# One decoder block in fp32: convolution taps loaded in rows of 512 bytes, latent columns split 352 and 352, last sums first on VectorE

## The chip, the cores and the metric

The kernel runs on one core of one Trainium2 chip. The metric is the device time of one execution in microseconds, the median over the runs. On the core, TensorE (PE) multiplies, VectorE (DVE), ScalarE (ACT) and GpSimd (POOL) do elementwise work, and SyncE (SP) issues the DMAs that bring data from HBM.

## The reference

One decoder layer on 512 tokens of width 1024, all in float32. An adaptive norm makes `h` from `x`; one input projection of `h` yields the columns of the GLU (2 x 1024), the latents of attention (384 for q, 256 for k and v, 64 for the rotary key, together 704) and the gates of the two branches (2 x 1024). Branch A is GLU, causal depthwise convolution with 31 taps, layer norm, swish and a projection; branch B is latent attention with eight heads. Both are gated, added and projected by `w_out`. Then comes an MLP of width 4096.

```
mod = silu(c) @ W_ada + b_ada                    # shift, scale, gate, twice
h = rms_norm(x, g_pre_mix) * (1 + scale1) + shift1
z = h @ w_in
u_glu, q_lat, kv_lat, k_r, gate_logits = split(z)
u = ua * sigmoid(ub)
u = causal_depthwise_conv(u, conv_w, conv_b)     # conv_w: 31 x 1024
y_a = silu(layer_norm(u)) @ w_conv_out
q = rms_norm(q_lat) @ w_uq ; kv = rms_norm(kv_lat) @ w_ukv
y_b = attention(q, kv, rope(k_r)) @ w_attn_out
y = (sigmoid(g_A) * y_a + sigmoid(g_B) * y_b) @ w_out
x = x + gate1 * rms_norm(y, g_post_mix)
h = rms_norm(x, g_pre_mlp) * (1 + scale2) + shift2
x = x + gate2 * rms_norm(square(relu(h @ w_mlp_in)) @ w_mlp_out, g_post_mlp)
```

## The kernel before

Each fp32 product is made of three matmuls in a faster format (`mm3`): every operand is split into a high half (a cast, on ScalarE) and a low half (the difference, on VectorE), and TensorE adds high x high, high x low and low x high. High and low halves lie in one large SBUF tile, `r_arena`; raw fp32 data, weights just loaded among it, lie in another, `f_arena`. Places in both are taken and given back during the kernel, so a load can only be issued when the data that had its place before has been used. The results of TensorE go through eight PSUM banks.

No instruction is issued where it is written. A planner records all of them, computes their dependences and orders each engine's queue, and `issue` sends them out, so nearly all instructions have line L388 in the profile. TensorE follows the program order. The other queues, SP's DMAs included, go by due time: an instruction's due time comes from the matmuls that depend on it, less costs on the way, and `plan.hurry` pulls those recorded under it forward (`HG` is 3e3, in ns). The key is

```
return (o.rank, o.i) if o.eng == "pe" else (o.dead - o.hurry, o.i)
```

Buffer places are chosen over eight passes from the times of the last plan. Any change of a cost or a size can so move rows in other places. DMAs share a ring of eight semaphores: the ninth waits for the landing of the first.

The stages in order: the adaLN vectors and the first projection, group by group over the input rows (`first_products`, groups k=0 to 7); eight transposes of the taps `cwr` into `cw`, which has channels on partitions; the latents (`lat_gemm`); the GLU tiles; attention over eight heads, with 240 tap multiply-adds of the convolution between its steps on VectorE (`pump`); the projection of attention; layer norm; the projections of both branches; the gates; `w_out`; the MLP in four chunks, each with a second gemm after Strassen, whose products the function `banked` adds into accumulators in `f_arena`; the last norm and the output. Late adaLN rows (`w_ada`) are accumulated on VectorE during layer norm and `w_out`.

In `lat_gemm` weights come in units (`wunit`: a DMA, a cast, a subtraction). The first 512 columns take four units of 2 x 512, in four open banks, one for each block of 128 tokens; the other 192 take two units of 4 x 192, one block after the other.

Of the kernel before, what the change touches and what calls it, by code (L numbers as in the profile page):

```python
# [15 lines left out]
ALU = mybir.AluOpType  # L16
# [376 lines left out]
def tile_hybrid_block(  # L393
# [48 lines left out]
    def emit(past, replay):  # L442
# [122 lines left out]
        pos4 = tile_of([NT, P], I32, "pos4")  # L565
        pos4f = tile_of([NT, P], F32, "pos4f")
        sp.dma_start(out=pos4, in_=positions[0].rearrange("(a p) -> a p", p=P))
        cwr = fa.alloc(D)
        sp.dma_start(out=fa.v(cwr)[:TAPS, :], in_=conv_w)
        plan.hurry = 0.0  # L570

        bc = pb.alloc()
# [53 lines left out]
        def hs(k, a=0, n=T):  # L626
            return ra.v(hT[k][0])[:, a:a + n], ra.v(hT[k][1])[:, a:a + n]
# [96 lines left out]


        cw = tile_of([P, KD, TAPS], F32, "cw")
        for ct in range(KD):
            pe.transpose(pb.v(bc)[:, 128 + ct * 32:128 + ct * 32 + TAPS], fa.v(cwr)[:TAPS, ct * P:(ct + 1) * P],
                         ident[:TAPS, :TAPS])
        dve.tensor_scalar(cw, pb.v(bc)[:, 128:384].rearrange("p (a b) -> p a b", b=32)[:, :, :TAPS], 0.5, None, ALU.mult)  # L730
        fa.free(cwr)
        pb.free(bc)

# [84 lines left out]
        kraw = fa.alloc(NT * DR)  # L818

        def lat_gemm():  # L820
            lb = [pb.alloc() for _ in range(NT)]
            for k0 in range(0, KD, 2):
                w = wunit(w_in, k0, C_QL, 2, 512)
                for k in range(2):
                    for t in range(NT):
                        mm3(pb.v(lb[t]), hs(k0 + k, t * P, P), w(k, 0, 512), k0 + k == 0, k0 + k == KD - 1)
                w.free()
                pump(PUMPS[0])
            for t in range(NT):
                b = fa.alloc(640)  # L830
                act.copy(fa.v(b)[:, 0:512], pb.v(lb[t]))
                latF.append(b)
            pb.free(*lb)
            ws = [wunit(w_in, kh, C_R2, 4, 192) for kh in (0, 4)]
            for t in range(NT):
                b = pb.alloc()
                for k in range(KD):
                    mm3(pb.v(b, 192), hs(k, t * P, P), ws[k // 4](k % 4, 0, 192), k == 0, k == KD - 1)
                act.copy(fa.v(latF[t])[:, 512:640], pb.v(b, 128))
                act.copy(fa.v(kraw)[:, t * DR:(t + 1) * DR], pb.v(b, 192)[:, 128:192])  # L840
                pb.free(b)
            for w in ws:
                w.free()
            pump(PUMPS[0])
# [678 lines left out]
        for ch in range(NCH):  # L1523
            hid = fa.alloc(HPC * T)
            hv = fa.v(hid, "p (k t) -> p k t", k=HPC)
            GRP = 4 if ch == 0 else 2
            for n0 in range(0, HPC, GRP):
                bs = [pb.alloc() for _ in range(GRP)]
                ws = ws0 if ch == 0 and n0 == 0 else hid_weights(ch * HPC + n0, GRP)
                step = 256 if ch == 0 and n0 == 0 else T  # L1530
                for t0 in range(0, T, step):
                    for i in range(GRP):
                        for k in range(KD):
                            mm3(pb.v(bs[i])[:, t0:t0 + step], ws[i - i % 2, k // 4](k % 4, (i % 2) * P, P), h2s(k, t0, step),
                                k == 0, k == KD - 1)
                for w in ws.values():
                    w.free()
                for i in range(GRP):
                    r = fa.alloc(T)
                    act.activation(fa.v(r), pb.v(bs[i]), AF.Relu)  # L1540
                    act.activation(hv[:, n0 + i], fa.v(r), AF.Square)
                    fa.free(r)
                    pb.free(bs[i])
                if ch >= NCH - 2:
                    take(late, ADAS[1])
            if ch == NCH - 1:
                for p_ in h2:
                    ra.free(*p_)
                take(late)
                G2 = gate_row(5, g_post_mlp, 1.0)  # L1550
                fin = [stat(4) for _ in range(NT)]
            if ch == 0:
                ysb = [fa.alloc(D) for _ in range(NT)]
            seen = {}

            def banked(mi, nh, bs):
                n = seen[mi, nh] = seen.get((mi, nh), 0) + 1
                done = n == (1 if (mi, nh) == (1, 0) else 2)
                sl = slice(nh * 512, (nh + 1) * 512)
                for tt in range(2):  # L1560
                    t = 2 * mi + tt
                    y = fa.v(ysb[t])[:, sl]
                    if ch == 0 and n == 1:
                        act.copy(y, pb.v(bs[tt]))
                    else:
                        dve.tensor_tensor(y, pb.v(bs[tt]), y, ALU.add)
                    if ch < NCH - 1 or not done:
                        continue
                    s = fin[t]
# [65 lines left out]
```

## Time and profile before

| | |
|---|---|
| median of 3 runs | 834.04 us (833.59 to 836.13) |
| profiled execution | 832.68 us |
| its span, first to last instruction | 830.9 us |
| granted TensorE clock, mean | 0.994 |
| TensorE busy | 805.1 us, 97% |
| VectorE busy | 686.6 us, 83% |
| ScalarE busy | 422.4 us, 51% |
| data moved by DMA | 117.28 MB, mean 141 GB/s |

Busy time is the time in which the engine executes; the rest of the span it waits. The profile names, for each wait, the instruction of another engine that ended last before it (the releaser). In the timeline a row is a start, a length, the engine, the operation and the count of equal ones, and in brackets the idle time before them. In the window view each engine has its busy time and count in the window; then come the granted clock, the mean busy share of the 16 DMA engines and the rate.

### The profile page before, as it was taken

Reading aid. Unit: us, or ns where it says so; the run is one execution under the profiler, and the core shown is the slowest. Engines: PE = TensorE matmul, PEld = TensorE weight load, DVE = VectorE, ACT = ScalarE, POOL = GpSimd, SP = SyncE. Lnnn points to the kernel's source line nnn. Section 1 sums busy time; section 2 is a strip of 40 time slices with the busy share of each in tenths; the row PEclk is TensorE's granted clock in tenths of the full one; section 3 lists DMA queues with packets and bytes.
Section 4 is the critical chain, followed back from the end, with each engine's and each line's share of the span. In section 5 each row is a group of like instructions: output and inputs, shape, how many; then the busy total and the mean of one; then the engine's idle time right before and its main releaser. Section 6 shows DMA issues by size and latency. Waiting matters only on the chain.

```text
span 830.9 us, 10647 instructions
## 1 busy us (share of the span) xinstructions
PE 805.1 (97%) x3940; PEld 672.5 (81%) x3940; DVE 686.6 (83%) x1012; ACT 422.4 (51%) x712; POOL 26.4 (3%) x84
## 2 busy tenths in 40 slices
PE   6989999999999999999999989999999999999995
PEld 3867888889987888888877879888888888888884
DVE  4979989999999999998999589298529993975696
ACT  5364273275884356218424387375346354554642
POOL 2001020000000000000000020000000000000001
PEclk9999999999999999999999999999999999999998
DMA  9998423201464140062799362065014831660302
GB/s 309 321 301 261 153 70 95 71 27 44 135 176 116 40 126 26 26 229 76 277 341 374 118 205 79 27 195 160 0 51 149 277 131 52 193 212 1 102 0 103
DMA packets 86824, 117.28 MB, mean 141 GB/s; under 512 B 7275, under 2 KB 60628, under 8 KB 86771
## 3 DMA queue, kind: packets, MB, share of 16 engines
q1 hardware_dynamic: 86770, 116.59, 43.6%
q8 instruction: 31, 0.51, 0.2%
q14 instruction: 23, 0.18, 0.1%
HBM read 108.18 MB, written 8.39 MB: 140 GB/s over the span
## 4 chain that ended last, share of the span: by engine, by line
PE 87%; DVE 6%; DMA 4%; ACT 2%; issue 1%; POOL 0%; POOLq 0%; DVEq 0%; ACTq 0%; SPq 0%
PE psum L388 87%; DVE f_arena L388 4%; DMA f_arena<-in_w_in_dram 2%; DVE r_arena L388 1%; ACT f_arena L388 1%; DMA f_arena<-in_w_out_dram 1%; ACT r_arena L388 1%; POOL stats L388 0%; DMA f_arena<-in_x_dram 0%; DMA f_arena<-in_w_ada_dram 0%; ACT stats L388 0%; POOLq L1630 0%; DVE mod L388 0%; DVEq L1630 0%; DVE cols L388 0%
## 5 line engine op out<-in xcount | busy, mean ns | idle before, releaser
L388 PE MATMUL psum<-r_arena 128*128 128x512 f32 (+3 forms) x3592 | 765.7, 373 | 8.5 <-ACT r_arena L388 3.6
L388 PEld LDWEIGHTS psum<-r_arena 128*128 128x128 f32 x3592 | 631.3, 189 | 126.8 <-ACT r_arena L388 4.9
L388 DVE TENSOR_TENSOR r_arena<-f_arena,r_arena 128x1024 fp32r<-128x1024 f32 (+4 forms) x232 | 248.1, 1093 | 97.2 <-PE psum L388 56.2
L388 ACT CAST r_arena<-f_arena 128x1024 fp32r<-128x1024 f32 (+4 forms) x222 | 209.3, 967 | 189.7 <-PE psum L388 123.5
L388 DVE SCALAR_TENSOR_TENSOR f_arena<-f_arena,cw 128x512 f32<-128x512 f32 x240 | 164.5, 748 | 0.0
L388 ACT ACTIVATE f_arena<-psum 128x512 f32<-128x512 f32 x64 | 38.1, 598 | 131.4 <-PE psum L388 124.6
L388 DVE TENSOR_TENSOR f_arena<-f_arena 128x1024 f32<-128x1024 f32 (+3 forms) x78 | 77.3, 1006 | 5.5 <-ACT f_arena L388 3.6
L388 ACT ACTIVATE f_arena<-f_arena 128x512 f32<-128x512 f32 (+3 forms) x100 | 58.5, 606 | 13.5 <-DVE f_arena L388 12.6
L388 DVE SCALAR_TENSOR_TENSOR f_arena<-f_arena,cT 128x256 f32<-128x256 f32 (+2 forms) x84 | 55.3, 705 | 0.2
L388 PE MATMUL psum<-ident,f_arena 128*128 128x128 f32 (+1 forms) x240 | 34.4, 283 | 7.5 <-DVE f_arena L388 7.5
L388 PEld LDWEIGHTS psum<-ident,f_arena 128*128 128x128 f32 (+1 forms) x240 | 28.9, 146 | 12.8 <-DVE f_arena L388 8.2
L388 DVE TENSOR_TENSOR f_arena<-psum,f_arena 128x512 f32<-128x512 f32 x52 | 35.4, 687 | 4.4 <-PE psum L388 4.3
L388 ACT CAST r_arena<-psum 128x512 fp32r<-128x512 f32 (+2 forms) x57 | 30.3, 567 | 16.6 <-PE psum L388 16.4
L388 DVE TENSOR_TENSOR r_arena<-psum,r_arena 128x512 fp32r<-128x512 f32 (+2 forms) x57 | 35.7, 658 | 2.5 <-ACT r_arena L388 1.9
L388 POOL TENSOR_TENSOR stats<-stats,nhalf 128x1 f32<-128x1 f32 x24 | 16.8, 708 | 485.4 <-ACT stats L388 485.4
L388 ACT COPY f_arena<-psum 128x512 f32<-128x512 f32 (+4 forms) x42 | 19.9, 501 | 22.1 <-PE psum L388 21.9
L388 ACT ACTIVATE r_arena<-f_arena 128x512 fp32r<-128x512 f32 (+3 forms) x20 | 13.0, 648 | 18.7 <-DVE f_arena L388 16.2
L388 DVE CUSTOM_DVE_ANT_0 f_arena<-psum,mask 128x128 f32<-128x128 f32 (+3 forms) x32 | 15.2, 487 | 2.6 <-PE psum L388 2.5
L388 DVE SCALAR_TENSOR_TENSOR f_arena<-f_arena 128x512 f32<-128x512 f32 (+1 forms) x18 | 13.4, 747 | 0.3
L388 DVE SCALAR_TENSOR_TENSOR f_arena<-f_arena,psum 128x512 f32<-128x512 f32 x16 | 11.0, 685 | 3.1 <-PE psum L388 2.6
L388 DVE TENSOR_SCALAR f_arena<-f_arena,stats 128x1024 f32<-128x1024 f32 x8 | 6.0, 752 | 8.4 <-POOL stats L388 8.4
L388 DVE SCALAR_TENSOR_TENSOR f_arena<-psum,stats,f_arena 128x512 f32<-128x512 f32 x8 | 5.6, 748 | 8.5 <-POOL stats L388 8.3
(94 smaller groups left out, 188.0 us busy)
## 6 DMA issues: line engine op xcount, KB each, us to landing
f_arena<-in_w_ada_dram SPq DMA_DIRECT2D x16, 1024.0 KB, 8.2
f_arena<-in_w_mlp_in_dram SPq DMA_DIRECT2D x32, 512.0 KB, 4.3
f_arena<-in_w_mlp_out_dram SPq DMA_DIRECT2D x32, 512.0 KB, 5.2
f_arena<-in_w_in_dram SPq DMA_DIRECT2D x28, 512.0 KB, 4.7
f_arena<-in_x_dram SPq DMA_DIRECT2D x8, 512.0 KB, 8.0
f_arena<-in_w_ada_dram SPq DMA_DIRECT2D x16, 256.0 KB, 5.7
f_arena<-in_w_ada_dram SPq DMA_DIRECT2D x8, 512.0 KB, 6.4
h_spill<-r_arena SPq DMA_DIRECT2D x16, 256.0 KB, 4.1
```

The source lines that it names most:

```text
L388: getattr(self.real[o.eng], o.fn)(*o.a, **o.k)
```

## The change

Three edits.

The taps, 31 rows of 1024 floats, are read as 248 rows of 128 floats (512 bytes) by three DMAs, of 112, 128 and 8 rows. The buffer has 256 words per partition and no longer 1024. Two transposes (128 x 128 and 128 x 120) take the place of eight (31 x 128), and the scaling into `cw` reads them in another stride.

The 704 latent columns are done as 352 and 352: four units of 2 x 352 for each half.

In the last chunk of the MLP, what `banked` records has `plan.hurry` at `HG`; the body moves to `add_block`, unchanged.

```
-        cwr = fa.alloc(D)
-        sp.dma_start(out=fa.v(cwr)[:TAPS, :], in_=conv_w)
+        cwr = fa.alloc(2 * P)
+        cw_rows = conv_w.rearrange("t (a p) -> (t a) p", p=P)
+        for r0, r1, at in ((0, P, 0), (P, P + 112, 0), (P + 112, TAPS * KD, 112)):
+            c0 = P if r0 else 0
+            sp.dma_start(out=fa.v(cwr)[at:at + r1 - r0, c0:c0 + P], in_=cw_rows[r0:r1])
...
-        for ct in range(KD):
-            pe.transpose(pb.v(bc)[:, 128 + ct * 32:128 + ct * 32 + TAPS], fa.v(cwr)[:TAPS, ct * P:(ct + 1) * P],
-                         ident[:TAPS, :TAPS])
-        dve.tensor_scalar(cw, pb.v(bc)[:, 128:384].rearrange("p (a b) -> p a b", b=32)[:, :, :TAPS], 0.5, None, ALU.mult)
+        for i, n in enumerate((P, TAPS * KD - P)):
+            pe.transpose(pb.v(bc)[:, (1 + i) * P:(1 + i) * P + n], fa.v(cwr)[:n, i * P:(i + 1) * P], ident[:n, :n])
+        dve.tensor_scalar(cw, pb.v(bc)[:, P:P + TAPS * KD].rearrange("p (b a) -> p a b", a=KD), 0.5, None, ALU.mult)
...
+            NL = (QL + KL + DR) // 2
...
-                w = wunit(w_in, k0, C_QL, 2, 512)
+                w = wunit(w_in, k0, C_QL, 2, NL)
...
-            ws = [wunit(w_in, kh, C_R2, 4, 192) for kh in (0, 4)]
+            ws = [wunit(w_in, kh, C_QL + NL, 2, NL) for kh in range(0, KD, 2)]
...
             def banked(mi, nh, bs):
+                plan.hurry = HG if ch == NCH - 1 else 0.0
+                add_block(mi, nh, bs)
+                plan.hurry = 0.0
```

The planner's order changes with it. Three places matter here.

First SP's queue at the first projection, where the taps are loaded. `in_conv_w_dram` are the taps; the loads of 128x4x128 are the weights of groups k=6 and k=7, those of 128x4x256 GLU weights, those of 128x2x512, 128x4x192 and 128x2x352 latent weights. Before:

```order
L388 DMA pos_96<-in_positions_dram 4x128
L388 DMA f_arena<-in_conv_w_dram 31x1024
L388 DMA f_arena<-in_w_in_dram 128x4x128 x2
L388 DMA f_arena<-in_w_in_dram 128x2x512 x3
L388 DMA f_arena<-in_w_in_dram 128x4x192
```

After, with the tap load of 112 rows standing some 25 rows further up:

```order
L388 DMA pos_96<-in_positions_dram 4x128
L388 DMA f_arena<-in_conv_w_dram 128x128
L388 DMA f_arena<-in_conv_w_dram 8x128
L388 DMA f_arena<-in_w_in_dram 128x4x256
L388 DMA f_arena<-in_w_in_dram 128x4x128 x2
L388 DMA f_arena<-in_w_in_dram 128x4x256
L388 DMA f_arena<-in_w_in_dram 128x2x352 x4
```

The one tap load became three, and a GLU load moved ahead of the weights of k=6 and k=7.

Second SP's queue ahead of the `w_out` gemm. `in_x_dram` is the residual, `in_w_ada_dram` a late adaLN load. Before:

```order
L388 DMA f_arena<-in_x_dram 128x1024
L388 DMA f_arena<-in_w_ada_dram 128x2x1024
L388 DMA f_arena<-in_x_dram 128x1024 x2
L388 DMA f_arena<-in_w_out_dram 128x2x512
L388 DMA f_arena<-in_w_ada_dram 128x2x1024
L388 DMA f_arena<-in_w_out_dram 128x2x512
```

After:

```order
L388 DMA f_arena<-in_x_dram 128x1024
L388 DMA f_arena<-in_w_out_dram 128x2x512
L388 DMA f_arena<-in_w_ada_dram 128x2x1024
L388 DMA f_arena<-in_x_dram 128x1024 x2
L388 DMA f_arena<-in_w_out_dram 128x2x512
L388 DMA f_arena<-in_w_ada_dram 128x2x1024
L388 DMA f_arena<-in_w_out_dram 128x2x512
```

The first `w_out` load moved ahead of one adaLN load and two residual loads, and the others follow earlier by about one place.

Third VectorE's queue at the end. A sum from `psum` into the accumulator is one of the gemm's last; a row with `stats` is a norm's last product. Before:

```order
L388 TENSOR_TENSOR f_arena<-psum,f_arena 128x512 x2
L388 TENSOR_TENSOR f_arena<-f_arena 128x512
L388 SCALAR_TENSOR_TENSOR f_arena<-f_arena,stats 128x512 x2
L388 TENSOR_TENSOR f_arena<-f_arena 128x512
L388 SCALAR_TENSOR_TENSOR f_arena<-f_arena,stats 128x512 x2
L388 TENSOR_TENSOR f_arena<-psum,f_arena 128x512
```

After:

```order
L388 TENSOR_TENSOR f_arena<-psum,f_arena 128x512
L388 SCALAR_TENSOR_TENSOR f_arena<-f_arena,stats 128x512 x2
L388 TENSOR_TENSOR f_arena<-f_arena 128x512
L388 SCALAR_TENSOR_TENSOR f_arena<-f_arena,stats 128x512 x2
L388 TENSOR_TENSOR f_arena<-psum,f_arena 128x512 x2
L388 TENSOR_TENSOR f_arena<-f_arena 128x512
```

The last sum from `psum` stood behind the norm of two other token blocks and now stands right behind the sum before it.

More of the change, by code (lines that the diff above doesn't have):

```diff
@@ L820, in lat_gemm @@
         def lat_gemm():
+            NL = (QL + KL + DR) // 2
             lb = [pb.alloc() for _ in range(NT)]
             for k0 in range(0, KD, 2):
-                w = wunit(w_in, k0, C_QL, 2, 512)
+                w = wunit(w_in, k0, C_QL, 2, NL)
                 for k in range(2):
                     for t in range(NT):
-                        mm3(pb.v(lb[t]), hs(k0 + k, t * P, P), w(k, 0, 512), k0 + k == 0, k0 + k == KD - 1)
+                        mm3(pb.v(lb[t], NL), hs(k0 + k, t * P, P), w(k, 0, NL), k0 + k == 0, k0 + k == KD - 1)
                 w.free()
@@ L829, in lat_gemm @@
             for t in range(NT):
-                b = fa.alloc(640)
-                act.copy(fa.v(b)[:, 0:512], pb.v(lb[t]))
+                b = fa.alloc(QL + KL)
+                act.copy(fa.v(b)[:, 0:NL], pb.v(lb[t], NL))
                 latF.append(b)
             pb.free(*lb)
-            ws = [wunit(w_in, kh, C_R2, 4, 192) for kh in (0, 4)]
+            ws = [wunit(w_in, kh, C_QL + NL, 2, NL) for kh in range(0, KD, 2)]
             for t in range(NT):
@@ L837, in lat_gemm @@
                 for k in range(KD):
-                    mm3(pb.v(b, 192), hs(k, t * P, P), ws[k // 4](k % 4, 0, 192), k == 0, k == KD - 1)
-                act.copy(fa.v(latF[t])[:, 512:640], pb.v(b, 128))
-                act.copy(fa.v(kraw)[:, t * DR:(t + 1) * DR], pb.v(b, 192)[:, 128:192])
+                    mm3(pb.v(b, NL), hs(k, t * P, P), ws[k // 2](k % 2, 0, NL), k == 0, k == KD - 1)
+                act.copy(fa.v(latF[t])[:, NL:QL + KL], pb.v(b, QL + KL - NL))
+                act.copy(fa.v(kraw)[:, t * DR:(t + 1) * DR], pb.v(b, NL)[:, QL + KL - NL:])
                 pb.free(b)
@@ L1556, in banked, with add_block @@
             def banked(mi, nh, bs):
+                plan.hurry = HG if ch == NCH - 1 else 0.0
+                add_block(mi, nh, bs)
+                plan.hurry = 0.0
+            def add_block(mi, nh, bs):
                 n = seen[mi, nh] = seen.get((mi, nh), 0) + 1
```

## The prediction

> **What bounds the kernel now.** I read the page's first and fourth part, then the waits of TensorE, then the timeline round each wait. Busy time and the chain of waits come first.
>
> ```profile
> PE 805.1 (97%) x3940; PEld 672.5 (81%) x3940; DVE 686.6 (83%) x1012; ACT 422.4 (51%) x712; POOL 26.4 (3%) x84
> ...
> PE 87%; DVE 6%; DMA 4%; ACT 2%; issue 1%; POOL 0%; POOLq 0%; DVEq 0%; ACTq 0%; SPq 0%
> ...
> PE psum L388 <- ACT r_arena L388: 3.6, 3, 2.4
> PE psum L388 <- DVE r_arena L388: 2.4, 4, 0.9
> ```
>
> TensorE carries 87% of the chain. So only three things shorten the kernel: fewer or shorter matmul slots, a wait of TensorE that goes, and the stretch after the last matmul. The two waits quoted are those the change can reach; the rest of this text finds where they stand. The profiled execution took 832.68 us, 1.36 below the median of the runs (834.04); the sum is made against 832.68 and 1.36 is added at the end.
>
> **Latent columns, 512 and 192 made into 352 and 352.** The rows give what one matmul costs back to back.
>
> ```profile
> L388 PE MATMUL psum<-r_arena 128*128 128x192 f32 x96 | 10.9, 274 | 0.0
> ...
> 492.24 7.68 PE L388 MATMUL psum<-r_arena 128*128 128x256 f32 x62
> ...
> 783.34 38.25 PE L388 MATMUL psum<-r_arena 128*128 128x512 f32 x168
> ```
>
> The first row is from the groups by shape, the others are of the timeline (start, length, count). 512 columns: 38.25/168 = 228 ns. 256: 7.68/62 = 124 ns. 192: 10.9/96 = 114 ns, hardly less than 256, so the narrow half pays for columns that it doesn't have. Before: 96 x 228 + 96 x 114 = 32.8 us. After: 192 matmuls of 352, a width that no row shows. Cheapest, in proportion to 512: 157 ns, 30.1 us (-2.7). Dearest, on the line from 192 to 512: 171 ns, 32.8 us (0). I take the line from 256 to 512, its nearest neighbours: 163 ns, 31.3 us, **-1.5 us**. All of it is on TensorE's path. The two extra weight units cost ScalarE and VectorE nothing new in bytes, only starts; VectorE's other work covers them, and if it didn't they would show as waits on r_arena in that gemm.
>
> **Tap transposes, eight made into two.**
>
> ```profile
> 70.80 0.67 PE L388 MATMUL psum<-ident,f_arena 31*128 31x31 f32 x8
> 71.40 1.89 PE L388 MATMUL psum<-r_arena 128*128 128x512 f32 x7
> ...
> 499.76 1.47 PE L388 MATMUL psum<-ident,f_arena 128*128 128x128 f32 x12
> ```
>
> The eight hold TensorE from 70.80 to 71.40, 0.60 us. Two full ones at 1.47/12 = 122 ns are 0.24: **-0.35 us** (bounds 0 and -0.4).
>
> **The tap load, one of 31 rows made into three of 112, 128 and 8.** The window view (busy times, then DMA share and GB/s last) and the timeline show the cost.
>
> ```profile
> 44.00:46.00 2.00, 1.94 (x8) 1.47 (x9) 2.00 (x8) 2.00 (x4) 0.00 (x0) 1.00 1.15 316
> 46.00:48.00 2.00, 2.00 (x12) 1.69 (x12) 2.00 (x6) 0.96 (x2) 0.00 (x0) 1.00 0.49 128
> 48.00:50.00 2.00, 2.00 (x10) 1.65 (x9) 2.00 (x9) 0.00 (x0) 0.00 (x0) 1.00 0.77 194
> ...
> 41.95 0.24 SPq L388 DMA_DIRECT2D f_arena<-in_conv_w_dram  x1
> 42.89 26.50 SPq L388 DMA_DIRECT2D f_arena<-in_w_in_dram  x16
> 53.08 0.62 ACT L388 CAST r_arena<-f_arena 128x512 fp32r<-128x512 f32 x1 [6.12 <-DMA f_arena<-in_w_in_dram]
> 55.91 0.50 PE L388 MATMUL psum<-r_arena 128*128 128x512 f32 x1 [0.69 <-DVE r_arena L388]
> 56.91 4.60 PE L388 MATMUL psum<-r_arena 128*128 128x512 f32 x19 [0.50 <-DVE r_arena L388]
> 60.47 1.05 ACT L388 CAST r_arena<-f_arena 128x1024 fp32r<-128x1024 f32 x1 [0.50 <-DMA f_arena<-in_w_in_dram]
> 62.28 0.50 PE L388 MATMUL psum<-r_arena 128*128 128x512 f32 x1 [0.78 <-ACT r_arena L388]
> 63.72 4.87 PE L388 MATMUL psum<-r_arena 128*128 128x512 f32 x20 [0.93 <-DVE r_arena L388]
> ```
>
> Right behind the taps the weights for group k=6 are issued (42.89) and land only when the cast begins at 53.08, 10 us later, though in between the engines are at 0.49 and 0.77 share. A few of them work while the others are empty: the taps' 124 KB go at a fraction of the rate, and each load queued behind has a part that must wait for them. At one sixteenth of 316 GB/s they would need 6.3 us. Meanwhile ScalarE stands 6.12 us in that cast with the scaling for k=6 and k=7 queued behind it, VectorE makes the low halves late, and TensorE waits 0.69 + 0.50 for k=6 and 0.78 + 0.93 for k=7: 2.90 us in gaps. The restarts add to it: a lone matmul holds 0.50 us where the stream spends 0.23, so about 0.27 at three of the four gaps, 3.7 in all.
>
> The Trainium skill ("DMA: Bandwidth & Descriptors", section "Why a DMA increments its semaphore by 16 and not by 1") says that such a load uses the largest number of engines up to 16 that divides its slowest dimension: 31 rows get one engine, 112 and 128 rows get 16, 8 rows get 8. At the page's rate for one engine 124 KB would be an estimated 4.4 us and not 6.3. The dip in the two windows agrees with one slow engine, though no row names it. By the rule alone rival C below would fall out; it keeps its chance because the rows show only the dip.
>
> After: 124 KB at 316 GB/s is 0.4 us. In the new order a 512 KB load for the GLU goes ahead of the k=6 weights (1.6 us at that rate). They should land at 53.1 - 6.3 + 0.4 + 1.6 = 48.8, before TensorE ends the group ahead of them (55.91 - 0.69 = 55.2), and the loads behind follow. Two more tap DMAs and two more latent ones lengthen SP's queue by four issues of about 0.4 us, in a stretch of 26.5 us for 16 where SP mostly waits for free semaphores. I take **-3.4 us** (bounds +1.6, if the GLU load only delays, and -3.7). Next to be late there is the casting of the latent units.
>
> **What the planner moves: the w_out loads.** The latent and tap edits change the planner's times and places, so later rows move too. The costly place is the start of the output gemm.
>
> ```profile
> 421.01 0.34 SPq L388 DMA_DIRECT2D f_arena<-in_x_dram  x1
> 425.67 0.38 SPq L388 DMA_DIRECT2D f_arena<-in_w_out_dram  x1
> 434.22 0.63 PE L388 MATMUL psum<-r_arena,onesr 128*128 128x512 f32 x2
> 436.19 1.57 ACT L388 CAST r_arena<-f_arena 128x1024 fp32r<-128x1024 f32 x2 [1.89 <-DMA f_arena<-in_w_out_dram]
> 437.29 1.20 PE L388 MATMUL psum<-r_arena 128*128 128x512 f32 x4 [2.44 <-ACT r_arena L388]
> 438.76 6.39 PE L388 MATMUL psum<-r_arena 128*128 128x512 f32 x20 [0.27 <-DVE r_arena L388]
> ...
> 440.00:450.00 10.00, 9.94 (x43) 7.78 (x43) 8.35 (x9) 5.51 (x6) 0.00 (x0) 0.89 1.06 378
> 434.00:480.00 46.00, 43.22 (x191) 34.73 (x190) 35.34 (x40) 17.50 (x33) 1.65 (x3) 0.96 0.69 243
> ```
>
> The first unit is issued at 425.67, cast at 436.19 (10.5 us later, with the engines full), and TensorE loses 2.44 + 0.27. Then 20 matmuls take 6.39 us where 20 x 228 ns are 4.55: 1.84 us at a lowered clock (0.89 in the window 440 to 450). Sum 4.55 us. In the new order the first w_out load stands directly behind the first x load, which went out at 421.01; the second takes about the old place of the first. By 10.5 us of flight the units are there at about 432 and 436; needed at 434.85 and, 24 matmuls later, 440.3. The margin is 3 to 4 us, so **-4.6 us** (bounds 0, and +1 if the x loads behind it come late for the residual). Three accumulations of the adaLN rows and several ada loads go behind the layer norm in return; VectorE has 35.3 us of work in the 46 us from 434 on, which covers them.
>
> The Trainium skill ("TensorE: Matmul & The Clock Gate", section "HAM oscillation — how this bites in real kernels") puts the clock loss at idle gaps above about 3.4 us. By that rule a gap of 2.44 us would cost only itself and this term would be -2.7 us; the measured 0.89 after it decides here.
>
> **The tail.** The last chunk's sums into the accumulators get priority on VectorE.
>
> ```profile
> 818.91 0.69 DVE L388 TENSOR_TENSOR f_arena<-psum,f_arena 128x512 f32<-128x512 f32 x1 [0.81 <-PE psum L388]
> 819.52 0.68 DVE L388 TENSOR_TENSOR f_arena<-f_arena 128x512 f32<-128x512 f32 x1
> 820.12 1.41 DVE L388 SCALAR_TENSOR_TENSOR f_arena<-f_arena,stats 128x512 f32<-128x512 f32 x2
> 821.44 0.69 DVE L388 TENSOR_TENSOR f_arena<-f_arena 128x512 f32<-128x512 f32 x1
> 822.04 1.41 DVE L388 SCALAR_TENSOR_TENSOR f_arena<-f_arena,stats 128x512 f32<-128x512 f32 x2
> 823.37 0.69 DVE L388 TENSOR_TENSOR f_arena<-psum,f_arena 128x512 f32<-128x512 f32 x1
> 825.98 1.41 DVE L388 SCALAR_TENSOR_TENSOR f_arena<-f_arena,stats 128x512 f32<-128x512 f32 x2 [0.44 <-POOL stats L388]
> ```
>
> The last matmul ends at 783.34 + 38.25 = 821.59, but its sum starts at 823.37 behind the other row block's products (1.78 us). Now the sum goes first, at 821.6. The statistics between it and the final products (2.61 us from 823.37 to 825.98) then partly overlap the other block's three products (821.44 and 822.04, 1.93 us), which end about 824.2: the final products start near 824.8, **-1.2 us** (bounds 0 and -1.8). A sum put ahead of a split could hold up TensorE, which has no gap in those 168 matmuls; that is the end at 0.
>
> **New waits.** VectorE carries the conv taps through the attention and is nearly full.
>
> ```profile
> L388 DVE SCALAR_TENSOR_TENSOR f_arena<-f_arena,cw 128x512 f32<-128x512 f32 x240 | 164.5, 748 | 0.0
> ...
> 300.00:350.00 50.00, 50.00 (x233) 41.05 (x232) 50.00 (x73) 22.11 (x48) 0.00 (x0) 1.00 0.17 46
> ...
> 360.39 0.75 DVE L388 TENSOR_SCALAR f_arena<-f_arena,cT 128x1024 f32<-128x1024 f32 x1
> 363.66 0.38 PE L388 MATMUL psum<-ident,f_arena 128*128 128x128 f32 x2
> ```
>
> The last tap ends before 360.39, TensorE's transposes for the norm stand at 363.66: 3.3 us of slack. TensorE now reaches them with fewer matmuls done (27 instead of 44 between them and the norm's sums, the rest put behind it), VectorE with three accumulations fewer. Counting both orders by the trace's durations leaves about 1.2 us. I charge one wait of the size of the small ones above, **+0.9 us** (bounds 0 and +4).
>
> **Sum:** -1.5 - 0.35 - 3.4 - 4.6 - 1.2 + 0.9 = -10.2; 832.7 - 10.2 = 822.5, with 1.4 for the median 823.9 us.
>
> **Rivals.** (A) The wait for w_out stays: the new order issues earlier, but the engines are at 1.06 share and the loads in front share them. Then 823.9 + 4.6 = 828.5. For it: 10 us of flight; against: 3 to 4 us of margin.
> (B) VectorE becomes the bound at the norm. It was 50.00 of 50 busy before; if 4 us more of its idle time fall into the attention, TensorE waits some 3 us beyond the slack, and a clock drop like the one at 438.76 adds 1.8: about 828.7. Against: three accumulations leave its path.
> (C) The tap load doesn't matter: k=6 is late from bandwidth alone, and the GLU load ahead adds 1.6. Then 823.9 + 3.4 + 1.6 = 828.9. Against: the dip to 0.49 share, which is the opposite of a lack of bandwidth.
> (D) Slower. In the attention the queue of VectorE is in order, so the softmax steps of a head stand behind taps of 0.75 us (the first row of the last fence); with the slack gone, three taps ahead of them at each of eight heads make 8 x 2.2 = 18 us: 842. It ends above the old time once each head waits over 1.3 us. Against: every wait of TensorE gives VectorE time to catch up, so eight in a row are unlikely.
>
> **How the numbers follow.** Forecast 0.52 (its own range 820.5 to 826.5), A 0.14, B 0.15, C 0.12, D 0.07. The latent and tail ends reach 820 below; A, B and C lie at 828 to 829, two of them together at 833. So 819.5 to 832. A difference of 0.3% (2.5 us) is about what these runs can tell from none. Faster 0.88, same 0.06 (two rivals together, or part of D), slower 0.06.
>
> **What the changed profile would show.** No dip of the DMA share near 46 to 50 and the rows of TensorE there without gaps; one group of 192 matmuls of 352 columns with 31.3 us; no wait of TensorE at the output gemm and PEclk 1.00 in it; under 8.5 us between the last matmul and the end of the span. What would make it wrong: a new wait of over 2 us on VectorE before the layer norm, or a cast of w_out still ended by its DMA with TensorE idle.

## The result and the profile after

The changed kernel takes 822.96 us (median of 4 runs, 820.72 to 826.2), the kernel before 833.82 (4 runs, 832.33 to 836.13). The ratio is 0.9876, 95% interval 0.984 to 0.9913. The profiled execution of the changed kernel took 821.15 us, its span is 819.4 (before 832.68 and 830.9). One run further down, of lat_split, took 1358.0 us at a mean granted clock of 0.56; it is left out there. First the page of the changed kernel: busy time, and the chain of waits.

```profile
PE 799.6 (98%) x3934; PEld 673.5 (82%) x3934; DVE 685.5 (84%) x1014; ACT 423.3 (52%) x714; POOL 28.5 (3%) x84
...
PE 95%; ACT 2%; DVE 1%; POOL 1%; DMA 0%; issue 0%; DVEq 0%; ACTq 0%
```

TensorE has 95% of the chain where it had 87%, and the 4% of DMA are gone. Its waits for r_arena, summed:

```profile
PE psum L388 <- ACT r_arena L388: 3.1, 3, 1.6
```

The line for VectorE's r_arena (2.4 us in four waits before) is gone. ScalarE's is nearly as long, but its three waits are others: the 2.44 us at `w_out` became 0.26, the 0.42 us in the first projection 1.28, and 1.58 us stand at the norms between `w_out` and the MLP, where TensorE waited for other work of ScalarE before (2.43 us, for `f_arena`). The places of the prediction, from the timeline of the changed kernel (start, length, count, and the wait with its releaser):

```profile
43.06 1.01 SPq L388 DMA_DIRECT2D f_arena<-in_conv_w_dram  x2
44.71 4.46 SPq L388 DMA_DIRECT2D f_arena<-in_w_in_dram  x8
44.81 2.39 PE L388 MATMUL psum<-r_arena 128*128 128x512 f32 x9 [1.28 <-ACT r_arena L388]
49.70 0.62 ACT L388 CAST r_arena<-f_arena 128x512 fp32r<-128x512 f32 x1 [2.00 <-DMA f_arena<-in_w_in_dram]
52.65 12.53 PE L388 MATMUL psum<-r_arena 128*128 128x512 f32 x54
67.82 0.38 PE L388 MATMUL psum<-ident,f_arena 128*128 128x128 f32 x2
67.96 4.32 PE L388 MATMUL psum<-r_arena 128*128 128x512 f32 x19
...
412.15 0.37 SPq L388 DMA_DIRECT2D f_arena<-in_w_out_dram  x1
434.91 1.20 PE L388 MATMUL psum<-r_arena 128*128 128x512 f32 x4 [0.26 <-ACT r_arena L388]
436.30 10.04 PE L388 MATMUL psum<-r_arena 128*128 128x512 f32 x43
...
479.45 0.96 PE L388 MATMUL psum<-r_arena 128*128 128x256 f32 x3 [1.58 <-ACT r_arena L388]
...
779.77 30.99 PE L388 MATMUL psum<-r_arena 128*128 128x512 f32 x136
810.80 0.69 DVE L388 TENSOR_TENSOR f_arena<-psum,f_arena 128x512 f32<-128x512 f32 x1 [0.90 <-PE psum L388]
813.93 1.41 DVE L388 SCALAR_TENSOR_TENSOR f_arena<-f_arena,stats 128x512 f32<-128x512 f32 x2
```

(The first row of the loads has the taps' 128 and 8 rows; the 112 rows went out earlier.) The cast of k=6 starts at 49.70 and no longer at 53.08, and the four gaps of TensorE at k=6 and k=7 are closed: 54 matmuls in one stretch. The first `w_out` load goes out at 412.15 (before 425.67), and the gemm starts after 0.26 us. At the end VectorE's last product ends at 815.34. The windows at the two places (busy time of TensorE, its weight loads, VectorE, ScalarE and GpSimd; then the granted clock, the DMA share and GB/s), and behind them the latent row of the groups by shape:

```profile
46.00:48.00 2.00, 2.00 (x13) 1.60 (x12) 2.00 (x8) 1.71 (x3) 0.00 (x0) 1.00 0.85 253
48.00:50.00 2.00, 2.00 (x10) 1.64 (x9) 2.00 (x9) 0.30 (x1) 0.00 (x0) 1.00 1.19 325
440.00:450.00 10.00, 10.00 (x45) 8.28 (x45) 10.00 (x11) 5.71 (x6) 0.00 (x0) 1.00 1.06 372
```

```profile
L388 PE MATMUL psum<-r_arena 128*128 128x352 f32 x192 | 30.8, 322 | 0.0
```

The dip of the DMA share to 0.49 is now 0.85, the granted clock in the `w_out` gemm 1.00 and no longer 0.89. 30.8/192 is 160 ns for a matmul of 352 columns.

### The profile page after: what moved, and what is told of

The parts are those of the page before. It is cut to its first block, busy times and chain, and to the rows that moved or that the text cites. A ratio compares the mean times of both kernels' runs of the same rounds, so it can differ in the third digit from the quotient of the medians.

```text
span 819.4 us, 10628 instructions
## 1 busy us (share of the span) xinstructions
PE 799.6 (98%) x3934; PEld 673.5 (82%) x3934; DVE 685.5 (84%) x1014; ACT 423.3 (52%) x714; POOL 28.5 (3%) x84
## 4 chain that ended last, share of the span: by engine, by line
PE 95%; ACT 2%; DVE 1%; POOL 1%; DMA 0%; issue 0%; DVEq 0%; ACTq 0%
PE psum L388 95%; DVE f_arena L388 1%; ACT f_arena L388 1%; POOL stats L388 1%; ACT r_arena L388 0%; DMA f_arena<-in_x_dram 0%; ACT stats L388 0%; DVEq L1639 0%; DVE mod L388 0%; ACTq L388 0%
## 5 line engine op out<-in xcount | busy, mean ns | idle before, releaser
L388 PE MATMUL psum<-r_arena 128*128 128x512 f32 (+2 forms) x3592 | 761.5, 372 | 3.2 <-ACT r_arena L388 3.1
L388 ACT ACTIVATE f_arena<-f_arena 128x512 f32<-128x512 f32 (+4 forms) x100 | 58.5, 604 | 18.6 <-DVE f_arena L388 17.4
L388 PE MATMUL psum<-ident,f_arena 128*128 128x128 f32 x234 | 34.9, 286 | 7.6 <-DVE f_arena L388 7.6
L388 PEld LDWEIGHTS psum<-ident,f_arena 128*128 128x128 f32 x234 | 28.8, 147 | 13.0 <-DVE f_arena L388 8.4
L388 POOL TENSOR_TENSOR stats<-stats,nhalf 128x1 f32<-128x1 f32 x24 | 20.1, 842 | 476.2 <-ACT stats L388 476.2
L388 ACT COPY f_arena<-psum 128x512 f32<-128x512 f32 (+5 forms) x42 | 19.8, 500 | 17.6 <-PE psum L388 17.6
L388 ACT ACTIVATE f_arena<-f_arena,lnh 128x512 f32<-128x512 f32 x16 | 12.2, 808 | 6.8 <-DVE f_arena L388 6.7
```

The costliest lines, as they stand in the source:

```text
L388: getattr(self.real[o.eng], o.fn)(*o.a, **o.k)
```

## Experiments

All ratios are to the kernel before, run beside it, from five rounds; in brackets the 95% interval. A kernel "with its order fixed" issues what the planner chose without the edit, so that nothing else moves.

**One edit alone: the taps.** The kernel before with the new tap loads and transposes.

```
-        sp.dma_start(out=fa.v(cwr)[:TAPS, :], in_=conv_w)
...
+            sp.dma_start(out=fa.v(cwr)[at:at + r1 - r0, c0:c0 + P], in_=cw_rows[r0:r1])
...
```

> The kernel before with the tap edit alone (three loads in rows of 512 bytes, two transposes). Theory 1 (a load of 31 rows runs on one DMA engine and holds up the loads queued behind it): TensorE's gaps at groups k=6 and k=7 go (2.9 us in gaps, 3.7 with restarts), the transposes save 0.45 us; the group of latent matmuls is unchanged at 32.8 us and the stretch after the last matmul at 9.3 us. Span -4 us from that alone; at the output gemm the planner puts the w_out loads in another order (three together behind two residual loads), so between 0 and -4.6 us more. Rival (the gain of the changed kernel in its first 70 us comes from the latent units being smaller and landing sooner): the gaps at k=6 and k=7 stay and the span falls by under 1 us there.

830.39 us, ratio 0.9974 (0.996 to 0.9988): less than expected. Its timeline:

```profile
47.23 1.19 PE L388 MATMUL psum<-r_arena 128*128 128x512 f32 x4 [1.74 <-ACT r_arena L388]
161.76 0.66 PE L388 MATMUL psum<-ident,f_arena 128*128 128x128 f32 x4 [1.70 <-DVE f_arena L388]
```

The gaps at k=6 and k=7 close, but TensorE now waits 1.74 us at group k=4, where the kernel before waits 0.42, and 1.70 us in the attention. At k=4 ScalarE's scaling stands behind a cast that waits for a load of adaLN weights until 45.52. The wait for `w_out` went too, which no line of this edit speaks of: the planner's order carries it.

**One edit alone: the latent columns.** The kernel before with 352 and 352.

```
-                w = wunit(w_in, k0, C_QL, 2, 512)
+                w = wunit(w_in, k0, C_QL, 2, NL)
...
-            ws = [wunit(w_in, kh, C_R2, 4, 192) for kh in (0, 4)]
+            ws = [wunit(w_in, kh, C_QL + NL, 2, NL) for kh in range(0, KD, 2)]
```

> The kernel before with the latent edit alone (352 and 352 columns). Theory 1: TensorE's gaps at k=6 and k=7 stay within 1 us of 2.9, since the taps still come as 31 rows; the latent matmuls take 30.8 us, 1.9 less. The w_out order here is that of the kernel before for the first unit (behind three residual loads), so by theory 2 (the wait at the output gemm is set by where the first w_out load stands in SP's queue) the wait there stays at 2 us or more, and the whole is -2 us. Rival to theory 2 (the wait went because TensorE or VectorE ahead of it shifted against each other by a microsecond or two): it changes here too, by more than 1 us.

823.99 us, ratio 0.991 (0.9894 to 0.9926): three quarters of the gain of the whole change. Its timeline:

```profile
62.10 4.83 PE L388 MATMUL psum<-r_arena 128*128 128x512 f32 x20 [0.70 <-DVE r_arena L388]
69.02 0.22 PE L388 MATMUL psum<-ident,pos4f 4*128 4x4 f32 x1 [0.79 <-DVE cols L388]
415.22 0.37 SPq L388 DMA_DIRECT2D f_arena<-in_w_out_dram  x1
```

The expectation had read the order wrongly: a `w_out` load does go out early, at 415.22, and the wait there is gone. One gap at k=7 (0.70 us) and one at the small transposes behind it (0.79) stay, as the slow taps are still there. Those at k=6 are gone: ScalarE has the scalings for k=6 ahead of the late cast, and TensorE came to this stretch 1.4 us later in this execution (k=4 starts at 45.49, before at 44.06). At the end the last sum stands first without any priority. The two edits share their gains: 1.9 and 8.3 us alone (the medians beside them, 832.32), 10.9 in the whole change.

**Only the `w_out` loads earlier.**

```
+            plan.hurry = 6e3
             w = wunit(w_out, k0, 0, 2, 512)
+            plan.hurry = 0.0
```

> The kernel before with one thing added: the first four w_out units are recorded with a hurry of 6e3, so that in SP's queue the first w_out load stands ahead of the first residual load and no longer behind three of them; the first 70 us are unchanged. Theory 2: the first unit is issued some 5 us earlier, the wait of 2.44 us and the lowered clock behind it go, the span falls by 4 to 5 us, with startup and tail as before. Rival (the DMA engines are full there, so earlier w_out loads only push others, and the wait moves to the norm after the gemm or to the MLP's weights): the first wait falls, but the span by under 2 us.

831.31 us, ratio 0.9995 (0.9981 to 1.001). The wait for `w_out` is gone, and the timeline shows what came:

```profile
418.18 1.20 PE L388 MATMUL psum<-r_arena 128*128 128x512 f32 x4 [0.91 <-ACT r_arena L388]
420.18 37.48 PE L388 MATMUL psum<-r_arena 128*128 128x512 f32 x164 [0.80 <-ACT r_arena L388]
487.65 0.66 PE L388 MATMUL psum<-ident,f_arena 128*128 128x128 f32 x4 [3.16 <-DVE f_arena L388]
```

Two waits one gemm earlier (`w_conv_out`), 1.71 us together, and 3.16 us at the norms between `w_out` and the MLP, where the kernel before waits 2.43. Behind that wait the granted clock was 0.87 from 490 to 500, so the loss at a lowered clock that stood at `w_out` came back there. So an earlier load does take that wait away, but by itself it pays for it at other places. In the changed kernel, and with either edit alone, the wait goes without such a price at `w_conv_out`; which of the moved rows makes the room isn't settled.

**The tap load on more engines, and nothing else.** The kernel before with its order fixed; the one load of 31 rows is issued as 16 and 15 rows.

```
+            if o is self.mark:
+                for r in (slice(0, 16), slice(16, 31)):
+                    self.real["sp"].dma_start(out=o.k["out"][r], in_=o.k["in_"][r])
+                continue
             getattr(self.real[o.eng], o.fn)(*o.a, **o.k)
```

> The kernel before with every queue in its old order and every buffer in its old place; the one tap load of 31 rows of 4 KB is issued as two, of 16 and of 15 rows, one behind the other. Theory 1 (one slow engine serves the load of 31 rows, and the weights of k=6 and k=7 queue behind it): the cast that waits for the weights of k=6 comes at 48 to 50 us and no longer at 53; TensorE's gaps at k=6 (0.69 and 0.50) go and those at k=7 (0.78 and 0.93) shrink by half or more, so 1.5 to 3 us less in the first 72 us, nothing elsewhere but what shifts at the output gemm. Rival (size of the rows or of the buffer, or the order of the queues): the cast moves by under 1 us and the span by under 0.5.

828.76 us, ratio 0.9965 (0.995 to 0.9981). Its windows, and behind them its timeline:

```profile
46.00:48.00 2.00, 2.00 (x12) 1.56 (x11) 2.00 (x8) 2.00 (x4) 0.00 (x0) 1.00 1.14 322
48.00:50.00 2.00, 2.00 (x10) 1.61 (x10) 2.00 (x7) 2.00 (x4) 0.00 (x0) 1.00 1.02 382
```

```profile
49.59 1.55 ACT L388 CAST r_arena<-f_arena 128x512 fp32r<-128x512 f32 x2
53.65 11.64 PE L388 MATMUL psum<-r_arena 128*128 128x512 f32 x50
433.02 1.19 PE L388 MATMUL psum<-r_arena 128*128 128x512 f32 x4 [1.62 <-ACT r_arena L388]
435.31 4.84 PE L388 MATMUL psum<-r_arena 128*128 128x512 f32 x20 [1.10 <-DVE r_arena L388]
```

No dip, no wait before the cast of k=6, no gap: the same bytes to the same places, only in two loads. In the trace of the kernel before the 31 packets of 4 KB come one after another, 206 ns apart or so, 6.2 us from the first's start (45.40) to the last's end (51.62); here they overlap and are through in 2.0 us. By the Trainium skill ("DMA: Bandwidth & Descriptors", section "Why a DMA increments its semaphore by 16 and not by 1") 31 rows go to one engine, 16 and 15 rows to 16 and 15; the trace agrees, with a time of 6.2 us for which the page's rate gave an estimated 4.4.

**The slow load put back.** The changed kernel with its order fixed, and ahead of the tap loads a copy that nobody reads.

```
+            if o is self.mark:
+                self.real["sp"].dma_start(out=self.extra[0][:, :D - 4], in_=self.extra[1][:, :D - 4])
             getattr(self.real[o.eng], o.fn)(*o.a, **o.k)
```

> The changed kernel with every queue in its order, and one useless copy of 31 rows of 4 KB (from HBM to HBM) put in SP's queue just ahead of the tap load of 128 rows. Theory 1: this is the old tap load without its data, so the weights of k=6 land 2 to 5 us later than in the changed kernel (cast at 49.7 there), TensorE's gaps at k=6 and k=7 return with 1 to 3.5 us. Rival: 124 KB more among 117 MB cost 0.4 us of the engines' time, so under 0.5 us.

827.80 us, ratio 0.9945 (0.993 to 0.9961). The timeline:

```profile
52.70 0.62 ACT L388 CAST r_arena<-f_arena 128x512 fp32r<-128x512 f32 x1 [4.74 <-DMA f_arena<-in_w_in_dram]
56.52 9.36 PE L388 MATMUL psum<-r_arena 128*128 128x512 f32 x40 [0.20 <-DVE r_arena L388]
68.59 0.22 PE L388 MATMUL psum<-ident,pos4f 4*128 4x4 f32 x1 [1.18 <-DVE cols L388]
130.00 29.36 PE L388 MATMUL psum<-r_arena 128*128 128x512 f32 x145 [1.35 <-DVE f_arena L388]
160.65 0.66 PE L388 MATMUL psum<-ident,f_arena 128*128 128x128 f32 x4 [1.29 <-DVE f_arena L388]
```

The copy's 31 packets go one after another, 5.8 us in all, and the late cast is back (4.74 us). TensorE then waits 0.20 us at k=6 and 1.18 us at the small transposes behind k=7, where VectorE is late: 1.4 us, near the low end of what was expected, and no gap at k=7 itself. The two waits in the attention, 2.64 us, are of another origin; the second run of the changed kernel, below, has them too, and by the time alone the two kernels can't be told apart.

**The middle: 128 rows read as 127 and 1.** The changed kernel, the first of its tap loads split so.

```
...
-        for r0, r1, at in ((0, P, 0), (P, P + 112, 0), (P + 112, TAPS * KD, 112)):
+        for r0, r1, at in ((0, P - 1, 0), (P - 1, P, P - 1), (P, P + 112, 0), (P + 112, TAPS * KD, 112)):
...
```

> The changed kernel with the tap load of 128 rows, which stands in SP's queue two places ahead of the weights of k=6, made into one of 127 rows and one of 1 row; all rows are still 512 bytes and the buffer, the transposes and the w_out order are those of the changed kernel. Theory 1: 127 rows go through one engine (64 KB, about half the old 124 KB), so the weights of k=6 land 2 to 3 us later than in the changed kernel and TensorE loses 0.5 to 2.5 us at k=6 and k=7 again. Rival (what counted is the size of the rows or of the buffer): nothing moves by more than 0.3 us.

825.25 us, ratio 0.992 (0.9902 to 0.9937). A miss: TensorE has no gap at k=6 or k=7. The 127 packets of 512 bytes do go one after another, but every 24 ns, and are through in about 3 us, half the time of the 31 rows of 4 KB. The weights of k=6 landed about 1 us later (5.5 us after their issue, 4.4 in the changed kernel), and the cast's slack hides that. The edit also changes the places of the tap loads in SP's queue: the 8 rows now go ahead of the 127, and the last row goes out at 53.22. Its difference to the changed kernel is of the size of that kernel's own spread.

**The tail, without and alone.** The changed kernel with `banked` as before:

```
...
-                plan.hurry = HG if ch == NCH - 1 else 0.0
-                add_block(mi, nh, bs)
-                plan.hurry = 0.0
```

> The changed kernel without the hurry on the last chunk's sums; TensorE's and SP's queues are the same as in the changed kernel, only the last 12 us of VectorE's differ, with the last sum behind the products of the other blocks again. Theory 3 (the hurry is what moved the last sum): 5.8 us from the last matmul to VectorE's last product, where the changed kernel has 4.6, and the span 0.5 to 0.8 us longer, since in the changed kernel the output's DMAs came 0.5 us nearer to each other and gave that back. Rival (the tail's gain is only the planner's other choices): no difference over 0.2 us.

824.01 us, ratio 0.99 (0.9884 to 0.9917). The end of its timeline:

```profile
779.63 33.94 PE L388 MATMUL psum<-r_arena 128*128 128x512 f32 x149
815.34 0.68 DVE L388 TENSOR_TENSOR f_arena<-psum,f_arena 128x512 f32<-128x512 f32 x1
817.95 1.42 DVE L388 SCALAR_TENSOR_TENSOR f_arena<-f_arena,stats 128x512 f32<-128x512 f32 x2 [0.44 <-POOL stats L388]
```

The old order: TensorE ends at 813.57, VectorE at 819.37, 5.80 us behind (4.58 with the priority). From there to the end of the span it is 9.1 us instead of 8.6: 0.5 us. The kernel before with these lines alone:

> The kernel before with the hurry alone. The planner moves sums of the last chunk that lie 10 to 30 us before the end, but its last eight rows on VectorE stay as before. So theory 3 expects here no gain: the stretch after the last matmul stays at 9.3 us, the span within 0.3 us. Rival (sums earlier anywhere free VectorE for the end): 0.5 us or more less after the last matmul.

832.45 us, ratio 1.0003 (0.9988 to 1.0018), and the tail is as it was. This kernel's start is that of the kernel before, instruction for instruction, and shows how far one execution differs from the next:

```profile
62.63 4.83 PE L388 MATMUL psum<-r_arena 128*128 128x512 f32 x20 [0.31 <-DVE r_arena L388]
68.74 0.22 PE L388 MATMUL psum<-ident,pos4f 4*128 4x4 f32 x1 [0.21 <-DVE cols L388]
```

Two gaps of 0.52 us together, where the profile before had four of 2.90. Part of that is where TensorE stood: it came to k=4 at 46.41 and not at 44.06, while the cast of k=6 came at 51.96, not later than before.

**The changed kernel once more.**

> The changed kernel once more, for more runs on one chip with the two that follow. The first four runs lay at 820.7, 821.2, 824.8 and 826.2 us. Theory 4: the spread is the clock (a window of 3.4 us at half speed that starts in some runs after the wait of 1.6 us near 478, worth 1.7 us) and the landing of the first small load near 9 us (worth 0.5 to 1.2 us). It expects runs at several levels within 820 to 826, a ratio of 0.986 to 0.991, and in a profile with clock 0.997 no half window near 480. Rival: the four runs differ by chip, and on one chip they agree within 1 us.

824.15 us (822.64 to 826.32), ratio 0.9916 (0.9893 to 0.994), a little outside the expected 0.986 to 0.991. The spread of 3.7 us on one chip is against the rival; the profile has no window at half speed, and what it does have is not in theory 4. The same program had two waits that its first profile doesn't have. Its timeline:

```profile
89.28 10.69 DVE L388 SCALAR_TENSOR_TENSOR f_arena<-f_arena,cw 128x512 f32<-128x512 f32 x16
92.79 8.13 POOL L388 TENSOR_TENSOR stats<-stats,nhalf 128x1 f32<-128x1 f32 x2 [23.04 <-ACT stats L388]
100.43 1.03 ACT L388 ACTIVATE f_arena<-f_arena,stats 128x384 f32<-128x384 f32 x2 [7.54 <-POOL stats L388]
106.72 1.23 DVE L388 TENSOR_TENSOR r_arena<-f_arena,r_arena 128x1024 fp32r<-128x1024 f32 x1 [6.75 <-ACT r_arena L388]
128.10 29.34 PE L388 MATMUL psum<-r_arena 128*128 128x512 f32 x145 [1.36 <-DVE f_arena L388]
158.76 0.66 PE L388 MATMUL psum<-ident,f_arena 128*128 128x128 f32 x4 [1.31 <-DVE f_arena L388]
```

Read downwards: GpSimd's two operations on one column take 8.13 us and end at 100.92, 0.95 us after VectorE's run of 16 taps; ScalarE waits for them, VectorE for ScalarE (6.75 us), and with VectorE that much later TensorE waits twice in the attention. In the first profile of the changed kernel it was the next pair, and a shorter stretch; it too ends 0.93 us after the taps:

```profile
89.17 10.68 DVE L388 SCALAR_TENSOR_TENSOR f_arena<-f_arena,cw 128x512 f32<-128x512 f32 x16
96.59 4.19 POOL L388 TENSOR_TENSOR stats<-stats,nhalf 128x1 f32<-128x1 f32 x2 [2.29 <-ACT stats L388]
103.22 1.23 DVE L388 TENSOR_TENSOR r_arena<-f_arena,r_arena 128x1024 fp32r<-128x1024 f32 x1 [3.37 <-ACT r_arena L388]
```

**The taps interrupted.** To see whether the taps are what holds GpSimd up:

```
...
+                if run == 2 and taps <= 60:
+                    self.real["dve"].tensor_scalar(self.pause[0], self.pause[1], 1.0, None, ALU.mult)
+                    run = 0
...
```

> The changed kernel with its order fixed, and behind every second conv tap of VectorE among the first 60 a product of 128x1 elements that nobody reads (20 of them, about 0.1 us each; the result stays the same). Theory 6: GpSimd's small operations on the statistics at 92 to 101 us stretched to 3.7 us (first profile of the changed kernel) or 7.6 us (second) because VectorE's run of 16 taps, each with two inputs from SBUF, keeps them out; a pause lets them in. Then no GpSimd operation there takes more than two taps (1.5 us) beyond its usual 0.5 to 0.9, ScalarE no longer waits 7.54 us for stats, the waits of 1.36 and 1.31 us of TensorE for VectorE near 130 and 160 us cannot appear, and the 2 us of pauses are hidden in VectorE's idle 3.4 us at 100 us: ratio to before 0.987 to 0.991. Rival: the stretch has another cause (the run as such, or GpSimd alone): an operation of 3.6 us or more is still there, and either the attention waits come or VectorE is 2 us later: ratio 0.991 to 0.995.

823.52 us (820.81 to 824.75), ratio 0.9898 (0.9876 to 0.992). The same place in its timeline:

```profile
93.31 1.39 POOL L390 TENSOR_TENSOR stats<-stats,nhalf 128x1 f32<-128x1 f32 x2 [23.04 <-ACT stats L390]
97.11 1.74 POOL L390 TENSOR_TENSOR stats<-stats,nhalf 128x1 f32<-128x1 f32 x2 [2.42 <-ACT stats L390]
101.30 1.23 DVE L390 TENSOR_TENSOR r_arena<-f_arena,r_arena 128x1024 fp32r<-128x1024 f32 x1
```

With a tiny product after every second tap no pair takes over 1.74 us, VectorE has no idle time at 101 us, and the waits in the attention aren't there. That is what theory 6 expects; it is one profile, and a stretch could be missing by chance, though one of 3.7 or 7.6 us was there in all six other profiles with the changed kernel's order at this place. The pauses break up the run of taps; that it is their second input from SBUF that counts was not tested. In time it can't be told from the changed kernel.

**The latent edit with the taps in two loads, and the last small wait.** First the kernel with the latent edit alone, its order fixed, and the lines of the 16 and 15 rows above:

> The kernel before with the latent edit, in the order that the planner makes for it, and with the one tap load of 31 rows issued as 16 and 15 rows in the same place. Theory 1: on top of the latent edit alone the waits of TensorE left at 61 us (0.98) and at 68 us (1.07) go, about 2 us; with the same start and clock its span is 819 to 820.5, as good as the changed kernel, though it has the old rows of 4 KB, the old buffer, eight transposes and no hurry. Rival (rows of 512 bytes or the smaller buffer matter besides): it stays 2 us behind the changed kernel.

822.36 us (median of five runs, 822.16 to 824.73), ratio 0.99 (0.9878 to 0.9922). The gaps at k=7 and behind it are gone; a wait of 0.72 us at `w_out` came. Its spans, 820.4 to 822.9, lie above the expected 819 to 820.5 for the most part. It can't be told from the changed kernel, though it has the old buffer and eight transposes. Then the changed kernel with its tap loads put later (`plan.hurry = -2e4` ahead of them), for the wait of 1.28 us at 44.81:

> The changed kernel with the three tap loads recorded with a negative hurry of 2e4: the load of 112 rows moves from its early place among the adaLN weights down to just ahead of the one of 128 rows, the one of 8 rows behind the latent weights; VectorE's and ScalarE's queues are unchanged. Theory 5: the wait of 1.28 us near 44 us (0.42 in the kernel before) comes from adaLN weights that land later behind the early tap load and the first-projection weights, so it shrinks to 0.4 to 0.9 and the span falls by 0.4 to 0.9 us. Rival: it comes from other loads moved ahead there (first-projection weights), and stays.

824.15 us, ratio 0.9914 (0.9892 to 0.9936). The wait is still 1.28 us: theory 5 falls. Its rival, other loads, isn't borne out either. In the kernel before this row stands between the small column products for k=4 (`psum<-ones,f_arena`) and the wait:

```profile
42.70 0.94 PE L388 MATMUL psum<-r_arena 128*128 128x512 f32 x3
```

From the end of the column products to the first matmul of k=4 it is 1.23 us before (42.83 to 44.06) and 1.28 after (43.53 to 44.81): VectorE and ScalarE need that long to make the scaled rows. Before, three matmuls fill most of it. In the changed kernel the planner has put them ahead of the column products, and TensorE has nothing to do meanwhile. All seven profiles with the changed kernel's order have the 1.28 us and not this row. So by the traces the wait comes from TensorE's own order (of the matmuls that the planner reckons ready it takes the first of the program, and which are ready changed) and not from a late load; no run puts the three matmuls back.

## Why the prediction held, point by point

It gave 823.9 us; the median is 822.96. Against the sum of -10.2 the median fell by 10.9 us and the profiled time by 11.5. That it came within 1 us is partly luck: run again beside the kernel before, the changed one gained 7.1 us (831.21 to 824.15), and the errors of the steps below cancel in part.

- **Latent columns: -1.5, measured -2.0** (32.8 to 30.8 us). 160 ns lie between the proportional 157 and the 163 of the line from 256 to 512.
- **Tap transposes: -0.35, measured -0.46** (67.82 to 67.96 are 0.14 us; before 0.60).
- **Tap load: -3.4.** The gaps of 2.90 us with their restarts are gone, and split_16_15 shows the cause by itself: 3.55 us from two loads in place of one (832.31 to 828.76; by the interval 1.6 to 4.2). So rival C is out. The size isn't fixed, though: from the start of k=4 to the end of the tap transposes it was 27.34 us in the profile before, 26.71 in wout_early and 23.98 in tail_only, all with the same start, and 23.10 in split_16_15. So the load cost 4.2, 3.6 and 0.9 us: the 3.4 us belong to the execution profiled before, not to each one.
- **`w_out`: -4.6, measured -4.3** (2.44 + 0.27 to 0.26 us of wait, and the 1.84 us of lowered clock, as the granted clock went from 0.89 to 1.00). Rival A is out. The first load went out at 412.15, earlier than the 421 of the step. The reason was only half right: in wout_early the load went out early too, and the time came back as waits elsewhere.
- **Tail: -1.2, measured -0.7.** VectorE ends 4.58 us after TensorE and no longer 5.80, which is the 1.2 of the step. The span behind the last matmul shrank only from 9.31 (830.9 - 821.59) to 8.64 us (819.4 - 810.76): the step left out the output's DMAs, which run on for 4.06 us behind VectorE's end where they ran for 3.51. It was predicted to be under 8.5 us. The edit did it: without it (no_tail) the 5.80 us are back.
- **New waits: +0.9, measured +0.75, but elsewhere.** The wait was charged at the layer norm, and there is none: TensorE runs from 357.09 to 367.71 without one, so rival B is out. The wait at k=4 grew from 0.42 to 1.28 us, of which 0.75 us are lost, as part of what TensorE did there before now comes earlier. That isn't the casting of the latent units, which the text named as next to be late; the three matmuls that filled the gap moved, and the prediction didn't look at TensorE's order there. It also left out the norms between `w_out` and the MLP, where the waits fell from 2.68 to 1.99 us. The attention's waits, 2.7 us, near the size that rival B looked for at the norm and rival D in every head, came in some executions only, and by way of GpSimd, which no step of the prediction watched.

## What to carry to other kernels

Look at the packets of a small load, and not at its bytes alone: one whose packets go one after another delays what is queued behind it (10.2 us from issue to landing for the weights behind the 31 rows, 4.4 in the changed kernel), and cutting 31 rows into 16 and 15 brought 3.55 us, where the tap edit alone, with the order that the planner made of it, brought 1.9. What counts is how long the series takes: 127 rows of 512 bytes, about 3 us, cost TensorE nothing. Where a planner sets the order, an edit's gain can lie far from the edit (the largest part of this one came at the output gemm, which no edit touches), and single edits don't add up. And read a second profile of the same program before a wait of 1 to 3 us is put down to an edit.

## What the runs showed of the hardware

**GpSimd behind VectorE.** An operation of GpSimd on 128x1 elements, usually 0.5 to 0.9 us, took up to 7.6 us while VectorE ran taps (two inputs from SBUF) back to back; the profile's spans on GpSimd are rough, but ScalarE's wait of 7.54 us bears this one out. The Trainium skill ("GPSIMD Engine Reference", section "1. Specifications") says that GpSimd shares its interfaces to SBUF with VectorE, with contention where a VectorE instruction has two inputs there; the runs agree, and show that a run of them can shut it out to its end. In each of the six profiles with the changed kernel's order and no pauses one of the two pairs was held so, the first (8.13 us) in two of them and the second (4.19 us) in four; the other got through in the midst of the run. Why it is now one and now the other isn't known.

**The clock after a short wait.** At 480 us the changed kernel and taps_pause have the same wait of 1.58 us, and then (windows of the first and of the second; the clock is third from the end):

```profile
480.00:490.00 10.00, 9.79 (x79) 9.39 (x80) 9.23 (x14) 9.73 (x19) 1.93 (x2) 1.00 0.79 250
```

```profile
480.00:490.00 10.00, 9.75 (x66) 9.33 (x67) 9.48 (x15) 9.77 (x19) 2.52 (x3) 0.83 0.82 251
```

0.17 of 10 us is 1.7 us of lost clock, 3.4 us at half speed, in one execution and not in the other. Of the seven profiles with this wait (1.58 to 1.60 us) four have such a window and three don't. The Trainium skill ("TensorE: Matmul & The Clock Gate", section "What's actually happening") gives a free-running window of 3413 ns; the length agrees. Its bound of about 3.4 us for a gap that matters doesn't: 1.58 us were enough here, and 1.62 and 1.10 us together were not in split_16_15 (4.84 us for 20 matmuls). Such a window (1.7 us) and the attention's waits (2.7) differ between executions of the same instructions, and with the old tap load the gaps at the start do too (0.52 to 2.90); that the first two make up all of the 5.5 us between the runs of the changed kernel wasn't shown.
